# A chunked recurrence's preparation: 64-row products and an inverse that starts from 8x8 blocks

## The chip, the cores and the metric

The kernel runs on one NeuronCore of a Trainium2 chip. A core has a matrix engine (TensorE, PE in the profile, with its weight loads as PEld), VectorE (DVE), ScalarE (ACT), GpSimd (POOL) and SyncE (SP), which here only issues DMAs. The engines work through queues of their own, each in order, and wait for one another by semaphores. The metric is the device time of one execution in microseconds (us); lower is better.

## The reference

Two layers of a hybrid encoder are applied to a prompt of 1024 tokens and to 8 running streams of 16 tokens each, all with 1024 channels. The first layer is an RWKV-7 time mixing, the second a forgetting attention, each followed by a squared-ReLU MLP and a layer norm. The change lies in the time mixing, whose recurrence is, per head (16 heads of 64 channels) and per token:

```
def step(S, inp):
    r_t, d_t, k_t, v_t, av_t, bv_t = inp
    sa = jnp.einsum('bhvk,bhk->bhv', S, av_t)
    S = S * d_t[:, :, None, :] + sa[..., None] * bv_t[:, :, None, :] + v_t[..., None] * k_t[:, :, None, :]
    y_t = jnp.einsum('bhvk,bhk->bhv', S, r_t)
    return S, y_t
...
S_fin, y = lax.scan(step, wkv0.astype(jnp.float32), (tmaj(r), tmaj(decay), tmaj(k), tmaj(v), tmaj(-kk), tmaj(kk * a)))
```

All of it is in float32. The kernel does not go token by token: it takes chunks of 64 tokens, in which the dependence of each token on those before it becomes a triangular system, I - G, of 64 x 64 for each head.

## The kernel before

The 1152 tokens are nine slabs of 128 (slab 0 holds the running streams, slabs 1 to 8 the prompt), two chunks of 64 to a slab. The work runs in three parts. First `project` computes what is local to a token; then comes the recurrence, in which the rest of the first layer for the first tiles runs beside it; then the remaining output product, the MLP, the attention and the second MLP. The change touches the recurrence alone.

For a slab `s` the recurrence has four steps, in functions inside `rwkv`:

- `prep(s)` loads the operands of both chunks. `CE` and `CO` hold the queries and the decayed keys of the even and the odd heads, `BK` what they are multiplied with; even heads lie in partitions 0 to 63 (`E_`), odd heads in 64 to 127 (`O_`). GpSimd clears the other half of `CE` and of `CO` (L449, L450), so that a product over all 128 rows of `BK` gives one head alone: L462, 32 matmuls of 128 columns to a slab, four to a PSUM bank `psG`, of which there are two. VectorE takes one half of a bank with a mask into `ABs` (L463), ScalarE the other half (L468), which GpSimd masks (L469). The even and odd rows of `BK` are then transposed on TensorE into `BT` (L475, out through ScalarE at L476).
- `inv(s)` inverts the 64 x 64 triangles of `ABs`: 32 of them in a slab. Each has four 16 x 16 blocks on its diagonal, 128 in all, one to a partition. VectorE turns them there with four 32x32-block transposes (L489), gathers them (L491, L492), and solves by substitution, 15 steps of a product (L500) and a sum (L501) over squares of 2 x 2 to 16 x 16. Two scalings (L504) and a transpose (L506) put the result back as blocks of 32 x 32 (`XD`; `XT` is its transpose, L511). For the prompt two merges on TensorE follow, each two products of the form X11 G12 X22: the first (L520, L522) fills the block above the diagonal of each 32 x 32 block in tiles of 32 x 32 rows and columns, the second (L546, L548) the same of the 64 x 64 blocks. Between them stand ScalarE copies (L525, L553, L555), a VectorE sum and transpose (L527, L529), and four copies back into `ABs`, two on GpSimd (L533) and two on ScalarE (L535). Slab 0 has blocks of 16 tokens and needs no merge.
- `chain(d, ...)` carries the state through a chunk with small matmuls (L581 to L609), using `CE`, `CO`, `ABs` and `BT`. Its PSUM banks `W0`, `U0`, `W1`, `U1` are the same four, one buffer each, that the merges of `inv` take (`psC`).
- `finish` norms and gates the output.

Beside them run `late` (called as `V(0)` to `V(2)`: values and gates, the matmuls at L34 to L36, L22 to L24 and L156 to L159 on `psA`) and the steps of `ahead` (output product and MLP for three tiles, on `psA` too), which take weights through ScalarE (L52) and VectorE or GpSimd (L53). The program is written in the order P(1), V(0), P(2), inv(1), C(1), inv(2), P(3), ... and a scheduler at compile time sets from this, from its own estimate of durations and from free buffers the order of each engine's queue. Tiles of the inverse share a pool tag `i` with three buffers.

## Time and profile before

| | |
|---|---|
| median of three runs | 3571.83 us (3569.07 to 3585.15) |
| span of the profiled execution, first to last instruction | 3573.1 us |
| PE busy in it | 3371.1 us, 94% |
| PEld busy | 3026.7 us, 85% |
| DVE busy | 1892.1 us, 53% |
| ACT busy | 1435.9 us, 40% |
| POOL busy | 1218.7 us, 34% |
| recurrence, about 425 to 1310 us of the span | 885 us |

The profile gives no separate time for the profiled execution beside its span; the span is 1.3 us over the median of the runs. A busy share is an average over parts with different limits, so it is the recurrence's own windows that count for this change. [...] A float32 matmul stands as two records in the trace, and a record's length includes its latency: what a matmul costs in a stream is the distance from start to start.

### The profile page before, as it was taken

How to read it: one execution, taken by the hardware profiler on the slowest of the kernel's cores; microseconds unless marked ns; L12 is line 12 of the kernel's file. 1: busy time of each engine (PE TensorE's matmuls, PEld its weight loads, DVE VectorE, ACT ScalarE, POOL GpSimd, SP SyncE). 2: the span in 40 equal slices, each digit the busy share in tenths (PEclk: the TensorE clock that was granted, in tenths of full speed). 3: DMA queues.
4: the chain of work that ended last, by engine and by line, in shares of the span. 5: the costliest groups of instructions: out<-in, count | busy, mean ns of one | idle time of the engine just before them, and what ended most of it. 6: DMA issues, size and time to landing. Idle time of an engine off the chain costs nothing.

```text
span 3573.1 us, 65174 instructions
## 1 busy us (share of the span) xinstructions
PE 3371.1 (94%) x26225; PEld 3026.7 (85%) x26225; DVE 1892.1 (53%) x3277; ACT 1435.9 (40%) x2906; POOL 1218.7 (34%) x1061
## 2 busy tenths in 40 slices
PE   7988978899999989999999999999989999999999
PEld 6877877888889888989988987787779899998887
DVE  8988698976674765332225144555456322222225
ACT  5555444443344433323323255555543333232222
POOL 6877765754543444111114011111104111111114
PEclk9988989998999999999999999999999999999999
DMA  4444764664443352212212323323441111111111
GB/s 130 141 137 133 203 165 113 169 184 122 115 119 104 105 198 91 72 59 65 66 59 83 117 74 105 119 90 110 138 150 48 59 48 36 48 45 44 42 42 62
DMA packets 287395, 358.18 MB, mean 100 GB/s; under 512 B 68690, under 2 KB 163948, under 8 KB 287092
## 3 DMA queue, kind: packets, MB, share of 16 engines
q1 hardware_dynamic: 285476, 353.21, 32.8%
q8 instruction: 206, 3.38, 0.4%
q0 software_dynamic: 1152, 0.69, 0.1%
q14 instruction: 97, 0.79, 0.1%
q10 hardware_dynamic: 464, 0.11, 0.0%
HBM read 293.83 MB, written 60.11 MB: 99 GB/s over the span
## 4 chain that ended last, share of the span: by engine, by line
PE 71%; DVE 13%; issue 5%; DMA 5%; POOL 3%; ACT 2%; SPq 1%; DVEq 0%; ACTq 0%; POOLq 0%
PE psy L22 6%; PE psy L24 6%; PE psy L23 6%; PE psz L24 6%; PE psz L23 6%; PE psz L22 6%; PE psA L22 4%; PE psA L23 4%; PE psA L24 4%; PE psO L1170 3%; DVE wl L53 2%; PE psT L1165 2%; PE psA L34 1%; PE psA L36 1%; PE psA L35 1%
## 5 line engine op out<-in xcount | busy, mean ns | idle before, releaser
L53 POOL TENSOR_TENSOR wl<-raw,wh 128x512 fp32r<-128x512 f32 (+1 forms) x291 | 400.1, 1376 | 1709.4 <-ACT wh L52 1656.7
L52 ACT ACTIVATE wh<-raw 128x512 fp32r<-128x512 f32 (+2 forms) x664 | 413.3, 626 | 1041.8 <-PE psy L24 441.4
L53 DVE TENSOR_TENSOR wl<-raw,wh 128x512 fp32r<-128x512 f32 (+2 forms) x373 | 315.9, 850 | 381.8 <-ACT wh L52 378.3
L22 PE MATMUL psz<-AH,wh 128*128 128x384 f32 x1280 | 432.5, 338 | 1.1 <-ACT AH L832 1.1
L24 PE MATMUL psz<-AH,wl 128*128 128x384 f32 x1280 | 432.1, 338 | 0.0
L23 PE MATMUL psz<-AL,wh 128*128 128x384 f32 x1280 | 431.9, 338 | 0.0
L22 PE MATMUL psy<-wh,hh 128*128 128x512 f32 x960 | 379.7, 396 | 0.2 <-DVE X L968 0.2
L24 PE MATMUL psy<-wh,hl 128*128 128x512 f32 x960 | 377.9, 394 | 0.0
L23 PE MATMUL psy<-wl,hh 128*128 128x512 f32 x960 | 377.8, 394 | 0.0
L970 DVE TENSOR_TENSOR X<-X,psy 128x512 f32<-128x512 f32 x210 | 143.9, 685 | 303.8 <-PE psy L24 303.8
L880 DVE TENSOR_TENSOR hl<-r,hh 128x384 fp32r<-128x384 f32 x192 | 115.7, 603 | 342.1 <-ACT hh L879 342.0
L22 PEld LDWEIGHTS psz<-AH,wh 128*128 128x128 f32 x1280 | 240.9, 188 | 2.4 <-ACT AH L832 1.8
L23 PEld LDWEIGHTS psz<-AL,wh 128*128 128x128 f32 x1280 | 241.1, 188 | 0.7
L24 PEld LDWEIGHTS psz<-AH,wl 128*128 128x128 f32 x1280 | 240.8, 188 | 0.0
L22 PE MATMUL psA<-AH,wh 128*128 128x384 f32 x624 | 220.1, 353 | 4.0 <-DVE i L501 2.7
L23 PE MATMUL psA<-AL,wh 128*128 128x384 f32 x624 | 217.4, 348 | 0.0
L24 PEld LDWEIGHTS psy<-wh,hl 128*128 128x128 f32 x960 | 180.4, 188 | 43.2
L22 PEld LDWEIGHTS psy<-wh,hh 128*128 128x128 f32 x960 | 180.5, 188 | 41.3 <-DVE X L968 0.6
L24 PE MATMUL psA<-AH,wl 128*128 128x384 f32 x624 | 214.6, 344 | 0.6 <-DVE wl L53 0.6
L23 PEld LDWEIGHTS psy<-wl,hh 128*128 128x128 f32 x960 | 180.4, 188 | 40.7
L22 PE MATMUL psA<-mh,wh 128*128 128x384 f32 x384 | 141.7, 375 | 38.4 <-DVE fac L323 16.4
L877 ACT ACTIVATE r<-psz 128x384 f32<-128x384 f32 x160 | 77.2, 483 | 185.2 <-PE psz L24 185.2
(390 smaller groups left out, 8466.4 us busy)
## 6 DMA issues: line engine op xcount, KB each, us to landing
raw<-m SPq DMA_DIRECT2D x336, 256.0 KB, 2.7
raw<-m2a SPq DMA_DIRECT2D x64, 256.0 KB, 2.7
sK<-ckT SPq DMA_DIRECT2D x16, 1024.0 KB, 5.5
sV<-cv SPq DMA_DIRECT2D x16, 1024.0 KB, 7.5
x<-xT SPq DMA_DIRECT2D x72, 192.0 KB, 3.4
raw<-w_r SPq DMA_DIRECT2D x48, 256.0 KB, 2.7
raw<-w_k SPq DMA_DIRECT2D x48, 256.0 KB, 2.7
raw<-w_v SPq DMA_DIRECT2D x48, 256.0 KB, 3.8
```

The lines of the kernel that those rows point to most:

```text
L22: nc.tensor.matmul(out, lh, rh, start=i == 0, stop=False)
L23: nc.tensor.matmul(out, lh, rl, start=False, stop=False)
L24: nc.tensor.matmul(out, ll, rh, start=False, stop=i == n - 1)
L34: nc.tensor.matmul(out, lh, rh, start=k == 0 and t % 2 == 0, stop=False, **kw)
L35: nc.tensor.matmul(out, lh, rl, start=False, stop=False, **kw)
L52: nc.scalar.activation(h, r, AF.Copy)
L53: lo[self.i % len(lo)].tensor_tensor(l, r, h.bitcast(F32), op=ALU.subtract)
L877: nc.scalar.activation(r, p, AF.Relu)
L880: nc.vector.tensor_tensor(l, r, h.bitcast(F32), op=ALU.subtract)
L970: nc.vector.tensor_tensor(xs, xs, p, op=ALU.add)
L1165: nc.tensor.transpose(p[:, j], Pms[e][:, (j0 + j) * 128 : (j0 + j) * 128 + 128], cst.ident)
L1170: nc.tensor.matmul(o[q, 0], V[:, j0 + j, q], PTs[e][:, j], start=j0 + j == 0, stop=j0 + j == i, skip_group_check=True)
```

## The change

In `prep` nothing is cleared any more. The products of the even and of the odd heads use the 64 rows of their own (`BK[b]` and `C[b]`), so each is a tile of 64 rows by 128 columns; two PSUM banks are taken at once, and the code issues the matmuls of even and odd heads by turns. The number of matmuls and their columns stay.

In `inv` the substitution starts from 8 x 8 blocks: 256 of them, two to a partition. The diagonal blocks of 32 x 32 are first copied out of `ABs` (`D1`, two copies on ScalarE, two on GpSimd), turned by two transposes of 128 partitions, and gathered in three steps. Seven substitution steps take both blocks of a partition at once. Four scalings and two transposes put the result back. A new merge, for slab 0 too, makes 16 x 16 blocks of them: GpSimd masks `D1` to the 8 x 8 blocks above the diagonal (`N8`), `XD` is transposed, two products of 64 matmuls each (32 x 32 rows and columns, 32 columns of data, four quadrants) run with a ScalarE copy between them, and VectorE adds the result into `XD`. The two merges of before follow unchanged.

```diff
-        rc = pc.tile([128, 578], F32, tag="rc", name="rc")
+        rc = pc.tile([128, 615], F32, tag="rc", name="rc")
         nc.sync.dma_start(rc, I.rconsts)
...
-        own = rc[:, 514:578]
-        mh = [rc[:, 512 + i : 513 + i] for i in range(2)]
+        own = rc[:, 512:576]
+        mh4, mle = ([rc[:, j + i : j + i + 1] for i in range(n)] for j, n in ((576, 4), (580, 3)))
+        m8 = rc[:, 583:615]
...
-                nc.gpsimd.memset(CE[O_], 0.0)
-                nc.gpsimd.memset(CO[E_], 0.0)
...
-                    for C, b, k in ((CE, E_, O_), (CO, O_, E_)):
-                        p = gps().rearrange("p (a b) -> p a b", a=4)
-                        for j in range(4):
-                            kb = hf * 4 + j
-                            nc.tensor.matmul(p[:, j], BK[:, kb], C[:, kb], start=j == 0, stop=j == 3, **kw)
+                    ps = [gps().rearrange("p (a b) -> p a b", a=4) for _ in range(2)]
+                    for j in range(4):
+                        for p, C, b in zip(ps, (CE, CO), (E_, O_)):
+                            nc.tensor.matmul(p[:, j], BK[b, hf * 4 + j], C[b, hf * 4 + j], start=j == 0, stop=j == 3, **kw)
+                    for p, C, b, k in zip(ps, (CE, CO), (E_, O_), (O_, E_)):
...
-            # (I - G)^-1 of the 16 x 16 blocks on the diagonal, a block to a partition
-            G1 = ti_((128, 16, 32))
             ABf = AB.rearrange("p c k t -> p (c k) t")
             qcol = [0, 32, 64, 96]
             qs = [slice(32 * q, 32 * q + 32) for q in range(4)]
+            turned = lambda t, v: t[:, v * 8 : v * 8 + 8].rearrange("p u (h t) -> p t h u", h=4)
+            D1 = ti_((128, 16, 32))
             for q in range(4):
-                nc.vector.transpose(G1[qs[q]], ABf[qs[q], :, qcol[q] : qcol[q] + 32].rearrange("p u (h t) -> p t h u", h=2))
-            Gt = pc.tile([128, 16, 16], F32, tag="Gt", name="Gt")
-            nc.vector.scalar_tensor_tensor(Gt.rearrange("p s t -> p t s"), G1[:, :, 0:16], mh[0], G1[:, :, 16:32], op0=ALU.mult, op1=ALU.add)
-            nc.vector.memset(Gt.rearrange("p a b -> p (a b)")[:, 0 : 256 : 17], 1.0)
-            X = ti_((128, 16, 16))
+                d = ABf[qs[q], :, qcol[q] : qcol[q] + 32]
+                if q % 2:
+                    nc.gpsimd.tensor_copy(D1[qs[q]], d)
+                else:
+                    nc.scalar.activation(D1[qs[q]], d, AF.Copy)
+            G1 = ti_((128, 2, 8, 32))
+            for v in range(2):
+                nc.vector.transpose(G1[:, v], turned(D1, v))
+            N8 = ti_((128, 16, 32))
+            nc.gpsimd.tensor_tensor(N8, D1, m8.unsqueeze(1).broadcast_to([128, 16, 32]), op=ALU.mult)
+            Gt, X = (pc.tile([128, 2, 8, 8], F32, tag=tag, name=tag) for tag in ("Gt", "Xs"))
+            tmp = pc.tile([128, 98], F32, tag="Ts", name="Ts")
+            Gv, Gs = Gt.rearrange("p v t s -> p (v t) s"), [G1.rearrange("p v t s -> p (v t) s")[:, :, i * 8 : i * 8 + 8] for i in range(4)]
+            for i in (2, 1, 0):
+                nc.vector.scalar_tensor_tensor(Gv, Gs[i], mle[i], Gs[3] if i == 2 else Gv, op0=ALU.mult, op1=ALU.add)
+            diag = lambda t: t.rearrange("p v a b -> p v (a b)")[:, :, 0:64:9]
             nc.gpsimd.memset(X, 0.0)
-            nc.gpsimd.memset(X.rearrange("p a b -> p (a b)")[:, 0 : 256 : 17], 1.0)
-            tmp = ti_((128, 256))
-            for s0 in range(14, -1, -1):
-                n = 16 - s0
-                tv = tmp[:, : n * n].rearrange("p (a b) -> p a b", a=n)
-                nc.vector.tensor_tensor(tv, X[:, s0:, s0:], Gt[:, s0, s0:].unsqueeze(1).broadcast_to([128, n, n]), op=ALU.mult)
-                nc.vector.tensor_reduce(X[:, s0:, s0 : s0 + 1], tv, axis=AX.X, op=ALU.add)
+            nc.gpsimd.memset(diag(X), 1.0)
+            for n in range(1, 8):
+                tv = tmp[:, : 2 * n * n].rearrange("p (v a b) -> p v a b", v=2, a=n)
+                r = slice(8 - n, 8)
+                nc.vector.tensor_tensor(tv, X[:, :, r, r], Gt[:, :, r, 7 - n].unsqueeze(2).broadcast_to([128, 2, n, n]), op=ALU.mult)
+                nc.vector.tensor_reduce(X[:, :, r, 7 - n : 8 - n], tv, axis=AX.X, op=ALU.add)
             X2 = ti_((128, 16, 32))
-            for h in range(2):
-                nc.vector.tensor_scalar(X2[:, :, h * 16 : h * 16 + 16], X, mh[h], None, op0=ALU.mult)
+            for h in range(4):
+                nc.vector.tensor_scalar(X2[:, :, h * 8 : h * 8 + 8], X.rearrange("p v t s -> p (v t) s"), mh4[h], None, op0=ALU.mult)
             XD = ti_((128, 16, 32))
-            nc.vector.transpose(XD.rearrange("p u (h t) -> p t h u", h=2), X2)
+            for v in range(2):
+                nc.vector.transpose(turned(XD, v), X2[:, v * 8 : v * 8 + 8])
             kw = dict(skip_group_check=True)
+            XT = ti_((128, 16, 32))
+            nc.vector.transpose(XT, XD)
+            Tm = None
+            for st in range(2):
+                p = cps(1 + 2 * st)
+                for u in range(16):
+                    for q in range(4):
+                        l, r = (N8, XT) if st == 0 else (Tm, XD)
+                        nc.tensor.matmul(p[qs[q], u * 32 : u * 32 + 32], l[qs[q], u], r[qs[q], u], start=u == 0, stop=u == 15, **kw)
+                pv = p.rearrange("p (a b) -> p a b", a=16)
+                if st == 0:
+                    Tm = ti_((128, 16, 32))
+                    nc.scalar.activation(Tm, pv, AF.Copy)
+                else:
+                    nc.vector.tensor_tensor(XD, pv, XD, op=ALU.add)
...
-    c = np.zeros((128, 578), np.float32)
+    c = np.zeros((128, 615), np.float32)
...
+    for i in range(4):
+        c[:, 576 + i] = p % 32 // 8 == i
+    for i in range(3):
+        c[:, 580 + i] = p % 32 // 8 <= i
+    s, t = (p % 32)[:, None], np.arange(32)[None]
+    c[:, 583:615] = (s // 16 == t // 16) & (s % 16 < 8) & (t % 16 >= 8)
```

The scheduler's orders differ from 1,894 matmuls into the program (the first preparation) to the last 4,991, which stand as before. Three places show how.

On VectorE, at the inverse of slab 1, there stood before (`ABs` and `Gt` as above, `xx`, `l`, `wl`, `f`, `wg` and `ev` belong to `late`):

```order
L489 STREAM_TRANSPOSE i<-ABs 32x512 x2
L127 TENSOR_SCALAR f<-f 32x384
L463 TENSOR_TENSOR ABs<-psG,rc 64x512
L145 TENSOR_TENSOR wg<-raw,wg 32x512
L489 STREAM_TRANSPOSE i<-ABs 32x512 x2
L491 SCALAR_TENSOR_TENSOR Gt<-i,rc 128x16x16
L492 MEMSET Gt 128x16
L105 COPY ev<-psA 128x256
L500 TENSOR_TENSOR i<-i,Gt 128x4
```

and now stands:

```order
L497 STREAM_TRANSPOSE i<-i 128x256 x2
L463 TENSOR_TENSOR ABs<-psG,rc 64x512
L504 SCALAR_TENSOR_TENSOR Gt<-i,rc 128x128
L504 SCALAR_TENSOR_TENSOR Gt<-i,rc,Gt 128x128
L463 TENSOR_TENSOR ABs<-psG,rc 64x512
L504 SCALAR_TENSOR_TENSOR Gt<-i,rc,Gt 128x128
L511 TENSOR_TENSOR Ts<-Xs,Gt 128x2
L463 TENSOR_TENSOR ABs<-psG,rc 64x512
L512 TENSOR_REDUCE Xs<-Ts 128x2
```

The inverse's own VectorE instructions go from 39 to 27 in a slab without its later merges, and those of `late` stand between them less often.

On TensorE, at the preparation of slab 1, there stood before (`CE` and `CO` are the even and the odd heads, `psA` is `late`):

```order
L35 MATMUL psA<-wl,h 128x256
L36 MATMUL psA<-wh,l 128x256
L462 MATMUL psG<-CE,BK 128x128 x4
L462 MATMUL psG<-CO,BK 128x128 x4
L462 MATMUL psG<-CE,BK 128x128 x4
L462 MATMUL psG<-CO,BK 128x128 x4
L475 MATMUL psG<-ct,BK 128x64 x8
```

and now stands:

```order
L461 MATMUL psG<-CE,BK 128x128 x4
L35 MATMUL psA<-wl,h 128x256
L36 MATMUL psA<-wh,l 128x256
L461 MATMUL psG<-CO,BK 128x128 x4
L461 MATMUL psG<-CE,BK 128x128 x4
L461 MATMUL psG<-CO,BK 128x128 x4
L475 MATMUL psG<-ct,BK 128x64 x16
```

The code's turns are not kept here: four even matmuls stand in a row, then four odd ones. Over the nine slabs an even matmul stands right beside an odd one, in either order, in 69 places of the queue (0 to 18 of them in a slab), where full turns would give about 280.

On TensorE, where the inverse of slab 1 comes in, there stood before the first merge (L520):

```order
L159 MATMUL psA<-wg,h 128x256
L462 MATMUL psG<-CE,BK 128x128 x4
L462 MATMUL psG<-CO,BK 128x128 x4
L462 MATMUL psG<-CE,BK 128x128 x4
L462 MATMUL psG<-CO,BK 128x128 x4
L475 MATMUL psG<-ct,BK 128x64 x16
L34 MATMUL psA<-wh,h 128x256 x2
L520 MATMUL psC<-i,ABs 32x16 x64
```

and now stand pieces of the new one (L529):

```order
L461 MATMUL psG<-CO,BK 128x128 x4
L529 MATMUL psC<-i 32x32 x6
L475 MATMUL psG<-ct,BK 128x64 x4
L156 MATMUL psA<-wh,h 128x256
L157 MATMUL psA<-wl,h 128x256
L158 MATMUL psA<-wh,l 128x256
L159 MATMUL psA<-wg,h 128x256
```

The new merge's first product stands before transposes of slab 2 and before matmuls of `late`, which can't pass it while it waits. Between its two products, and again before the next merge, some 15 to 34 other matmuls stand in most slabs. Over the recurrence, neighbours in TensorE's queue whose tiles differ in rows or columns go from 483 to 575.

## Rows read from the trace of the kernel before

**Rows 1.** The page: span.

```profile
span 3573.1 us, 65174 instructions
```

**Rows 2.** Windows: stretch, us, busy PE PEld DVE ACT POOL (instructions), PEclk, DMA share, GB/s.

```profile
425.00:1310.00 885.00, 805.46 (x10560) 734.87 (x10560) 661.39 (x1184) 372.63 (x744) 479.34 (x450) 0.93 0.49 137
463.00:729.00 266.00, 226.80 (x3464) 204.72 (x3464) 241.95 (x420) 113.92 (x242) 171.32 (x182) 0.87 0.54 147
729.00:1310.00 581.00, 548.02 (x6885) 502.99 (x6883) 394.90 (x732) 243.87 (x472) 278.62 (x237) 0.96 0.43 127
```

**Rows 3.** Windows of the inverses' substitutions: the first, and nine summed.

```profile
463.00:498.00 35.00, 21.77 (x149) 19.63 (x148) 33.68 (x59) 14.84 (x30) 26.64 (x29) 0.81 0.61 172
...
sum 372.00, PE 329.69 PEld 299.83 DVE 344.24 ACT 155.65 POOL 202.93; mean PE 36.63 PEld 33.31 DVE 38.25 ACT 17.29 POOL 22.55
```

**Rows 4.** Waits of PE, 463 to 729 us: total, times, longest.

```profile
PE psC L520 <- DVE i L511: 9.2, 4, 5.6
```

**Rows 5.** DVE groups of the inverse, 425 to 1310 us: count, busy, mean ns, idle before.

```profile
L500 DVE TENSOR_TENSOR i<-i,Gt 128x4 f32<-128x4 f32 (+4 forms) x135 | 61.5, 455 | 2.7
...
L489 DVE STREAM_TRANSPOSE i<-ABs 32x512 f32<-32x512 f32 x36 | 38.4, 1068 | 0.5
L501 DVE TENSOR_REDUCE i<-i 128x2 f32<-128x4 f32 (+4 forms) x135 | 34.4, 255 | 2.8
...
L506 DVE STREAM_TRANSPOSE i<-i 128x512 f32<-128x512 f32 x9 | 9.9, 1102 | 0.1
...
L491 DVE SCALAR_TENSOR_TENSOR Gt<-i,rc 128x256 f32<-128x256 f32 x9 | 8.9, 992 | 0.1
...
L504 DVE TENSOR_SCALAR i<-i,rc 128x256 f32<-128x256 f32 x18 | 8.5, 512 | 0.1
...
L511 DVE STREAM_TRANSPOSE i<-i 128x512 f32<-128x512 f32 x8 | 5.6, 698 | 0.1
```

**Rows 6.** Two of those groups by shape, 425 to 1310 us.

```profile
L500 DVE TENSOR_TENSOR i<-i,Gt 128x36 f32<-128x36 f32 x9 | 3.7, 410 | 0.2
...
L501 DVE TENSOR_REDUCE i<-i 128x6 f32<-128x36 f32 x9 | 1.7, 190 | 0.2
```

**Rows 7.** Timeline of PE at merges of slab 6: start, us, instruction.

```profile
1014.71 0.34 PE L24 MATMUL psA<-AH,wl 128*128 128x384 f32 x1
1014.98 1.26 PE L520 MATMUL psC<-i,ABs 32*32 32x16 f32 x128
1016.17 0.45 PE L22 MATMUL psA<-AH,wh 128*128 128x384 f32 x1
...
1024.47 1.31 PE L546 MATMUL psC<-i,ABs 32*32 32x32 f32 x64
```

**Rows 8.** Timeline of PE at a preparation.

```profile
486.68 1.16 PE L462 MATMUL psG<-CE,BK 128*128 128x128 f32 x8 [0.51 <-ACT CE L468]
487.71 1.16 PE L462 MATMUL psG<-CO,BK 128*128 128x128 f32 x8
```

**Rows 9.** Timeline of PE at transposes: both halves by turns, then one alone.

```profile
742.68 1.02 PE L475 MATMUL psG<-ct,BK 64*128 64x64 f32 x16
...
820.13 0.71 PE L475 MATMUL psG<-ct,BK 64*128 64x64 f32 x8
```

**Rows 10.** Timeline of PE where the tile's shape changes.

```profile
1046.49 0.28 PE L35 MATMUL psA<-wl,hh 128*128 128x256 f32 x1
1046.60 0.28 PE L36 MATMUL psA<-wh,hl 128*128 128x256 f32 x1
1046.81 0.46 PE L475 MATMUL psG<-ct,BK 64*128 64x64 f32 x4
```

**Rows 11.** Groups of POOL and ACT, 425 to 1310 us, columns as in rows 5.

```profile
L449 POOL MEMSET CE<- 64x1024 f32 x18 | 17.1, 948 | 1.0
...
L533 POOL COPY ABs<-i 32x512 f32<-32x512 f32 x18 | 12.2, 679 | 10.6 <-DVE i L527 6.0 <-DVE i L506 2.8 <-DVE st L631 1.0
...
L535 ACT ACTIVATE ABs<-i 32x512 f32<-32x512 f32 x18 | 11.3, 626 | 17.2 <-DVE i L527 13.3 <-DVE i L506 3.8
```

More of the change, by code (lines that the diff above doesn't have):

```diff
@@ L1411, in _prep @@
         c[:, i * 256 : i * 256 + 256] = np.concatenate([np.where(e, ab, ba), np.where(e, ba, ab)], 1)
-    for i in range(2):
-        c[:, 512 + i] = p % 32 // 16 == i
     t = np.arange(64)[None]
-    c[:, 514:578] = p[:, None] == t // 16 * 32 + t // 16 % 2 * 16 + t % 16
+    c[:, 512:576] = p[:, None] == t // 16 * 32 + t // 16 % 2 * 16 + t % 16
+    for i in range(4):
[4 more added lines that the diff above has]
+    c[:, 583:615] = (s // 16 == t // 16) & (s % 16 < 8) & (t % 16 >= 8)
     o["rconsts"] = c
```

## The prediction

> **What bounds the kernel now.** I looked first at the page's engine shares: TensorE is busy 94% of the 3573.1 us [rows 1], which says little, as the change touches the recurrence alone. So the windows come next. In the recurrence's 885 us TensorE is busy 805, 91%, at a mean clock of 0.93 [rows 2]. The reader is to see that this is a mean of two stretches with different limits. From 463 to 729 us, with four of the nine inverses, VectorE is busy 242 of 266 us (91%) and TensorE 227 (85%), at a clock of 0.87. TensorE loses there 39 us idle and about 0.13 x 227 = 29 us to the lower clock, 68 us in all, and VectorE is what it waits for. From 729 to 1310 us it is the other way round: TensorE 548 of 581 us (94%) at 0.96, VectorE 395 (68%). What is lost there is 33 us idle and 0.04 x 548 = 22 us of clock.
>
> Windows laid on the substitutions alone (from the first L489 to L506, nine of them) sum to 372 us, in which VectorE is busy 344, or 93%; in the first, TensorE has work for 22 of 35 us only, at a clock of 0.81 [rows 3]. The list of TensorE's waits names the inverse at its head: L520 waited 9.2 us in four places for the transpose L511 that ends it [rows 4]. The groups by line give the inverse's own VectorE time: 61.5 + 38.4 + 34.4 + 9.9 + 8.9 + 8.5 = 161.6 us, 18.0 us a slab [rows 5]. That is the largest single block on the engine that sets the early stretch.
>
> **The change part by part.** VectorE in the inverse. The four turns of 32 partitions x 512 (1.07 us each) become two of 128 x 256: half the columns, so I take 0.55 each, 1.1 us. Gathering: three steps of 128 columns; half of L491's 0.99 or of L504's 0.51 for 256 [rows 5], I take 0.4, together 1.2. Substitution: seven pairs over 2 to 98 elements; the pair at 36 elements takes 0.41 + 0.19 [rows 6], so 7 x 0.6 = 4.2, against (61.5 + 34.4)/9 = 10.7 before. Scalings 4 x 0.26 = 1.0, the two transposes back 1.1, the new transpose `XT` 0.7 as L511, the sum into `XD` over as many columns 0.7 too. That is 10.0 against 18.0: 8 us less a slab, 72 us in all. Bounds: were each halved piece to cost what the whole does, the four halved kinds would cost 2.1 + 3.0 + 2.0 + 2.2 and the slab 14.9, 3 us less (27 in all); were they as short as their sizes allow and the small substitution steps cheaper still, some 10 us less (94).
>
> TensorE, new merge: 18 products of 64 matmuls, 128 records each. No row shows 32 data columns in four quadrants, but two stand close. [...] L546, 32 columns in two quadrants, has 64 records in 1.31 us less the last one's latency, which I estimate at 0.19, so a quadrant is free again after 1.12/32 = 35 ns [rows 7]. Four records at L520's pace, 1.26 less that latency over 128 = 8.5 ns, fill just these 35 ns, so the product keeps L520's length: 18 x 1.29 = 23 us. Bounds: 0 where TensorE would have idled anyway, 46 where all of it falls to the lower clock.
>
> TensorE, 64-row products. A record of L462 takes 1.03/8 = 0.13 us [rows 8], and its columns don't change. Two tiles of 64 rows do run side by side: 16 transposes of both halves, partly by turns, take 1.02 us, where eight of one half take 0.71 and eight more at 0.06 would make 1.2 [rows 9]. But only neighbours gain. In the order there are 69 places where an even matmul touches an odd one, each worth one record: 69 x 0.13 = 9 us. Full turns would give some 36. On the other side each change of the tile's shape costs: L36 follows L35 after 0.11 us, the 64*128 transpose follows L36 after 0.21 [rows 10]. Of the 92 further changes about 36 belong to the new products and are in their 1.29; 56 x 0.1 = 6 us remain, since L462 had the shape of its neighbours and its successor hasn't. So the two-heads part is worth 3 us of TensorE, and the whole change adds about 20.
>
> [...]
>
> POOL and ACT. Four clearings of 0.95 us a slab go, 34 us in all; two copies of 0.68 [rows 11] and one mask of 512 columns come, which I put at 1.4, twice a copy of 32 x 512; about 1 us a slab less. ScalarE gets two copies of 0.63 and one out of PSUM of about 0.6: 1.9 a slab, 17 us. Both engines are busy around half of the recurrence [rows 2], so I count neither. If that cover is gone, it is the copies `D1` that show: 1.4 us at the head of each inverse, 12 us. The list behind rows 4 names no clearing among TensorE's waits, so its end ends no stall.
>
> The wait that is added: the first product of the merge waits for `XT`, the second for ScalarE's copy, the next merge for VectorE's sum. Behind each stand matmuls of `late` or `ahead` and, in slab 1, transposes of slab 2, on which ScalarE and then the next inverse wait. With 15 to 34 other matmuls in between, at about 0.12 us each, some 2 to 4 us cover a copy of 0.6 and a sum and transpose of 1.4, so I count nothing; uncovered it would be about 1 us a slab.
>
> The sum. Early stretch: VectorE's load falls by 4 x 8 = 32 us; TensorE at full clock needs 227 - 29 + 4 x 2.2 = 207 of the 266 and doesn't bind. Not all of the 32 comes through, as DMAs also hold this stretch (share 0.54), so two thirds: 22 us less, with the added TensorE work inside it. Late stretch: TensorE's 5 x 2.2 = 11 us come in full, and VectorE's 40 us get back a fifth of the 55 lost: 11. Net nothing. What is late next in the early stretch is the matmuls and weight loads of `late`. The profiled execution: 3573.1 - 20 = 3553 us; the median stands 1.3 lower, so 3552.
>
> **The rivals.**
> First: VectorE sets more than I think. Then the early 32 us come in full and the late stretch gains half of 40 less 11, so 41 us less: 3531. For it speaks the 93% in rows 3; against it TensorE's 94% late.
> Second: the change brings nothing to measure, since DMA and order hold the early stretch. With 10 us gained early and 11 lost late: 3573. For it: only one wait of 9.2 us is plainly the inverse's.
> Third, the slower side: TensorE is the bound and the new merge stands in its queue. The 20 us of added work land in full, and the waits of the new products, uncovered by about 1 us a slab, add 9: 3601. It decides from the point at which less than 20 us of the 68 us lost early comes back. For it: 91% busy over the recurrence, pieces of the new merge ahead of slab 2's transposes in the queue. Against it: the early stretch, where TensorE has slack.
> Fourth: the quadrants of the new merge don't run beside one another. Then a product takes 128 x 35 ns = 4.5 us, 18 x 3.4 = 61 us more than forecast: 3613.
>
> **How the numbers follow.** The forecast, 3552, has 0.45, with a range of its own from 3538 to 3566; the first rival 0.18, the second 0.20, the third 0.13, the fourth 0.04. 0.5% is 18 us, about what this kernel's runs differ by. Faster than 3554: all of the first, somewhat over half of the forecast and a little of the second, 0.46. Slower than 3590: most of the third and the fourth, 0.14. The rest, 0.40, is within. The range, 3522 to 3592, cuts off the lower fourth of the first rival and most of the third and fourth, under 2 in 10.
>
> **What would show it.** VectorE's lines of the inverse should sum to about 90 us instead of 162, most of it in the seven substitution steps. From 463 us on, the four early inverses and what goes with them should end some 22 us sooner, with TensorE's clock over 0.9. The new products should take about 1.1 us from first to last record at the full clock, and L461's even and odd records should start within 10 ns of each other only where the queue has them side by side. The forecast is wrong if TensorE waits over 1 us a slab at L529, if VectorE's 72 us are gone and the early stretch is as long as before, or if the late one shrinks.

## The result and the profile after

The changed kernel takes 3626.09 us (median of 4 runs, 3622.53 to 3628.2), the kernel before 3574.38 (4 runs, 3569.07 to 3585.15): a ratio of 1.0147, with an interval from 1.0129 to 1.0165. It is 52 us slower. The forecast was 3552 us, 3522 to 3592, and "slower" had the smallest chance.

The windows of the kernel after, over the stretches of [rows 2], columns as there:

```profile
425.00:1310.00 885.00, 813.85 (x12435) 731.52 (x12434) 584.89 (x1018) 373.77 (x734) 444.76 (x430) 0.85 0.45 129
463.00:729.00 266.00, 230.58 (x4339) 204.06 (x4339) 206.37 (x356) 110.61 (x229) 157.55 (x174) 0.77 0.48 136
729.00:1310.00 581.00, 550.21 (x7896) 497.83 (x7896) 353.68 (x629) 247.17 (x474) 262.52 (x226) 0.90 0.40 118
```

The trace records TensorE's granted clock at two levels, and PEclk is its mean over a stretch: 1.0 and 0.5 before, 0.949 and 0.5 in this one profile, where the others have 1.0 for the upper level; matmuls behind the recurrence last as long as before (338 ns for the 384 columns of `psz` in both). With that, the share of the early stretch at the lower level is (0.949 - 0.77) / 0.449 = 40%, where 0.87 before is 26%. VectorE has become lighter, 206 instead of 242 us. TensorE is busier and still gets less done, since it runs at the lower level for longer: by the record of the granted clock, 191 us of the recurrence instead of 123. The recurrence, from 425 us to the last matmul of its chain, takes 905 us instead of 856.

The first substitution, 20 us instead of the 35 of [rows 3]:

```profile
469.00:489.00 20.00, 14.88 (x77) 12.87 (x75) 19.27 (x33) 5.86 (x12) 18.81 (x24) 0.58 0.59 170
```

VectorE's groups of the new inverse, 425 to 1362 us (it was [rows 5]). They sum to 103.7 us instead of 161.6, with the sum into `XD` (L535) and the new transpose `XT` (L522) among them:

```profile
L511 DVE TENSOR_TENSOR Ts<-Xs,Gt 128x2 f32<-128x2 f32 (+6 forms) x63 | 28.7, 455 | 1.6
L512 DVE TENSOR_REDUCE Xs<-Ts 128x2 f32<-128x2 f32 (+6 forms) x63 | 12.2, 193 | 1.5
L515 DVE TENSOR_SCALAR i<-Xs,rc 128x128 f32<-128x128 f32 x36 | 11.9, 387 | 0.2
L504 DVE SCALAR_TENSOR_TENSOR Gt<-i,rc,Gt 128x128 f32<-128x128 f32 x18 | 11.8, 658 | 0.4
L497 DVE STREAM_TRANSPOSE i<-i 128x256 f32<-128x256 f32 x18 | 10.8, 632 | 4.9 <-POOL i L492 4.1 <-PE psC L576 0.7
L518 DVE STREAM_TRANSPOSE i<-i 128x256 f32<-128x256 f32 x18 | 10.2, 645 | 0.2
L522 DVE STREAM_TRANSPOSE i<-i 128x512 f32<-128x512 f32 x9 | 6.3, 697 | 0.0
L535 DVE TENSOR_TENSOR i<-psC,i 128x512 f32<-128x512 f32 x9 | 6.1, 683 | 2.6 <-PE psC L529 2.5
L504 DVE SCALAR_TENSOR_TENSOR Gt<-i,rc 128x128 f32<-128x128 f32 x9 | 5.7, 630 | 0.2
```

TensorE's timeline at one product of the new merge, and at a place where products of the two heads follow each other by turns. Two heads' records start together, and 0.11 us later the next two:

```profile
633.66 1.29 PE L529 MATMUL psC<-i 32*32 32x32 f32 x128
...
1100.34 0.27 PE L461 MATMUL psG<-CE,BK 64*128 64x128 f32 x1
1100.34 0.27 PE L461 MATMUL psG<-CO,BK 64*128 64x128 f32 x1
1100.45 0.27 PE L461 MATMUL psG<-CE,BK 64*128 64x128 f32 x1
1100.45 0.28 PE L461 MATMUL psG<-CO,BK 64*128 64x128 f32 x1
```

TensorE's waits at the preparation and the merges, 425 to 1362 us: total, times, longest. The first of the older merges no longer waits for the inverse's transpose, as L520 did for L511 [rows 4]; the products now wait for ScalarE's copies out of the banks (2.1 and 0.5 us before), and the older merges for their own copy (L553) and transpose (L557), once each:

```profile
PE psG L461 <- ACT CE L468: 9.7, 6, 2.6
PE psC L550 <- ACT i L553: 4.5, 1, 4.5
PE psC L574 <- DVE i L557: 4.3, 1, 4.3
PE psG L461 <- ACT CO L468: 3.7, 4, 2.0
...
PE psC L529 <- DVE Stmp L628: 0.3, 1, 0.3
```

Where the recurrence's 49 us come from can be added up by charging each TensorE record with the time from its start to the next one's, less waits, and taking half of what lies at the lower level as the clock's price (in the two kernels with streams below, 600 records of 64 rows take 67.26 us at a clock of 1.00 and 400 take 85.70 at 0.50, 112 and 214 ns each):

```
                                  before    after
new merge, at full clock             0       25.6
all other records, at full clock   725.8    723.8
half of the records' time at 0.5    54.3     84.9
waits                               76.2     71.2
```

So 26 us are the new merge, 31 us the clock, and waits and other records give 7 back. All that VectorE was spared gave TensorE almost no time.

### The profile page after: what moved, and what is told of

It is laid out like the page before. It is cut to its first block, busy times and chain, and to the rows that moved or that the text cites. A ratio compares the mean times of both kernels' runs of the same rounds, so it can differ in the third digit from the quotient of the medians.

```text
span 3626.4 us, 69718 instructions
## 1 busy us (share of the span) xinstructions
PE 3432.4 (95%) x28529; PEld 3070.1 (85%) x28529; DVE 1847.1 (51%) x3169; ACT 1455.7 (40%) x2933; POOL 1201.4 (33%) x1052
## 4 chain that ended last, share of the span: by engine, by line
PE 66%; DVE 6%; DMA 3%; issue 3%; POOL 1%; ACT 1%; SPq 0%; DVEq 0%; ACTq 0%; POOLq 0%
PE psy L22 6%; PE psy L24 6%; PE psy L23 6%; PE psz L24 6%; PE psz L23 6%; PE psz L22 6%; PE psA L23 3%; PE psA L22 3%; PE psA L24 3%; PE psO L1198 3%; PE psT L1193 2%; PE psA L34 1%; PE psA L36 1%; PE psA L35 1%; PE psS L1178 1%
```

## The experiments

Each version below is the kernel before or after with the edit shown. The first four weigh the merge (A) against the new preparation, with its two banks and its longer time at the lower clock (B). C then says that products of 64 rows keep the clock down; D, that the order and the two banks held together make the price; E, that it is the missing clearings. The table gives all timed versions. "Lower, all" is the time at the lower level in the whole kernel, (1 - mean granted clock) x span x 2, averaged over a version's runs (of the changed kernel without the one that records 0.949); "in rec." is the same by the clock's record of the profiled execution in the recurrence, and "waits" TensorE's there, so these two stand on one execution each.

```
version        rows cleared merge   ratio [95%]            lower,all in rec. waits
before          128  yes     no     1                       247-262   123     76
e14_bt128       128  yes     no     0.9977 [0.9967,0.9986]    216      96     79
e10_invonly     128  yes     left out 0.9971 [0.9956,0.9986]  242      96     68
e12_loaded      128  no      no     1.002  [1.001,1.003]      245     123     85
e5_rows128      128  yes     no     1.0065 [1.0047,1.0083]    268     143     86
e2_inv          128  yes     yes    1.0068 [1.0053,1.0083]    246     102     73
e3_nomerge       64  no      left out 1.0005 [0.9992,1.0017]  274     154     65
e9_cleared       64  yes     no     1.0046 [1.0031,1.0061]    315     171     82
e13_rows64c      64  yes     no     1.0098 [1.0081,1.0116]    317     212     77
e6_onebank       64  no      no     1.01   [1.0069,1.0131]    306     167     79
e1_prep          64  no      no     1.0123 [1.0106,1.014]     336     225     81
e15_after_bt128  64  no      yes    1.0101 [1.0079,1.0122]    286     150     72
after            64  no      yes    1.0147 [1.0129,1.0165]    324     191     71
e7_chained       64  no      yes    1.0162 [1.0147,1.0177]    321     198     91
e4_turns         64  no      yes    1.0404 [1.0387,1.0421]    416     266    162
```

**The two parts apart.** e1_prep is the kernel before with the changed preparation; e2_inv is the changed kernel with the preparation of before.

```diff
-for C, b, k in ((CE, E_, O_), (CO, O_, E_)):      # e1_prep: these go, and the clearings
-    p = gps()...; for j: matmul(p[:, j], BK[:, kb], C[:, kb], ...)
+ps = [gps()... for _ in range(2)]
+for j in range(4):
+    for p, C, b in zip(ps, (CE, CO), (E_, O_)):
+        matmul(p[:, j], BK[b, hf * 4 + j], C[b, hf * 4 + j], ...)
```

> The kernel before with the new preparation alone (64-row products, two banks at once, nothing cleared); the inverse is that of before. Even and odd matmuls touch in 74 places of its queue. Theory A (the price of the change is the new merge's TensorE time, start to start 35 us in the changed kernel's recurrence; the preparation is worth next to nothing): 3574 to 3584 us. Theory B (the price is the new preparation: products that wait for both banks, 11 us more in the changed kernel, and a longer time at the lower clock): 3595 us or more.

> The changed kernel with the preparation of before (128-row products of cleared halves); the inverse from 8x8 blocks stays. Theory A: 3605 to 3620 us, most of the 52 us. Theory B: under 3595 us. If the parts add up, this and the preparation alone sum to the 52 us.

e1_prep took 3617.95 us against 3574.45, e2_inv 3596.65. So the part forecast as 3 us of gain costs 43 by itself, the inverse 22; together they cost 52, less than the sum. For e2_inv neither theory's range fits. The early stretch of e1_prep (columns of [rows 2]) shows where: TensorE as busy as before, the clock at 0.72.

```profile
463.00:729.00 266.00, 228.58 (x3009) 201.25 (x3008) 212.10 (x386) 99.25 (x209) 133.34 (x154) 0.72 0.49 129
```

At full clock e1_prep's recurrence needs 720.2 us of TensorE instead of 725.8, the small gain that was forecast; half of its time at the lower level is 100.4 instead of 54.3.

**The merge.** e3_nomerge is the changed kernel without the 8x8 merge (its mask, transpose, products, copy and sum, so part of each 16 x 16 block of the inverse is left out); e10_invonly the same with the preparation of before.

```diff
-N8 = ...; XT = ti_(...); nc.vector.transpose(XT, XD)
-for st in range(2): ... matmul(p[qs[q], ...], l[qs[q], u], r[qs[q], u], ...) ...
```

> The changed kernel without the new merge of 8x8 blocks (mask, transpose, both products, the copy and the sum are left out, so the blocks of 16 are not complete and the output isn't the reference's). VectorE's shorter substitution stays. Theory A: the merge's 35 us of TensorE go, and its share of the lower clock: 3580 to 3592 us. Theory B: 3600 us or more. If VectorE's relief of 8 us a slab were worth what I had forecast, this would be under 3555 us.

> The kernel before with the inverse from 8x8 blocks and without its new merge on TensorE (so the 8x8 blocks below the diagonal are left out: part of the computation): VectorE's relief by itself, with the preparation of before. As the prediction's main forecast had it, that relief is worth 22 to 33 us when TensorE gets nothing more to do: 3540 to 3552. If TensorE is what sets the recurrence, it is worth almost nothing: 3565 to 3578. Together with the changed kernel's inverse on the same preparation (1.0068) it gives the merge's full price: 25 us if it is TensorE's time at full clock and nothing else.

e10_invonly is the test of VectorE's relief, and it is worth 9 us (3564.93 against 3574.22, by the interval 5 to 16), though without the merge's own transpose and sum VectorE is spared some 70 us, 161.6 to 91. Its early stretch has VectorE at 213 us instead of 242, but TensorE at 235 instead of 227:

```profile
463.00:729.00 266.00, 235.45 (x3709) 210.91 (x3710) 213.41 (x371) 127.06 (x264) 178.22 (x195) 0.90 0.53 153
```

The merge costs 1.0068 - 0.9971, about 35 us, with 128-row products, and 51 us with 64-row ones (3574.97 to 3626.09), though its records take 25 to 26 in both. With the 64 rows the merge brings 37 us more at the lower level of the recurrence (154 to 191), with 128 rows 6 more (96 to 102). e3_nomerge, at 3574.97, lies below both theories: the new preparation costs 12 us beside this inverse (1.0005 - 0.9971), 30 with the merge (3596.65 to 3626.09) and 43 beside the inverse of before.

**Turns.** e4_turns keeps each bank pair's eight matmuls together as one uninterrupted block; e7_chained only fixes their order of issue.

```diff
+with tc.tile_critical():                            # e4_turns, around the eight matmuls
+    prev = matmul(...), each issued after prev      # e7_chained
```

> The changed kernel with each bank pair's eight product matmuls kept in the turns of the code (one block for the scheduler): even and odd touch in 254 places instead of 69. If each place is worth a record (0.13 us), 24 us less of TensorE: 3602 us. If the turns put the halves side by side but the time is lost to the lower clock or to waits for two banks, 3615 to 3630 us.

> The changed kernel with one edit: the eight product matmuls of a pair of banks are queued in the written order (even, odd, even, ...) by an edge that sets the order of issue alone, so other work may still stand between them: 220 touching places instead of 69, and no blocks that wait as a whole. Theory C: the products cost some 25 us less TensorE time at full clock, but the time at the lower clock stays as long as in the changed kernel (191 us) or gets longer: 3595 to 3630. Theory D (the order is what costs): the price of the preparation goes with it, 3570 to 3590. If the waits of the blocks were what made the kernel with blocks slow (3718), this one is at least 80 us faster than that one under both.

Turns do save what they promise: the products' cost at full clock falls from 65.7 us to 39.6 in e4_turns (254 touching places) and to 51.9 in e7_chained (220). But e4_turns' block waits as a whole for things that have nothing to do with the preparation, as the head of its waits shows (425 to 1410 us), and e7_chained loses 20 us to more waits and stays as long at the lower level as the changed kernel. Both were slower than it, e7_chained within the intervals; e4_turns is far outside both of its forecasts.

```profile
PE psG L461 <- DMA raw<-g1b: 17.8, 1, 17.8
PE psG L461 <- POOL xx L78: 12.8, 2, 7.8
PE psG L461 <- DMA vg<-v: 9.6, 3, 5.3
```

**Rows, banks, clearings.** Five edits of the preparation of before.

```diff
e5_rows128:  both banks asked for together, matmuls by turns in the code, still BK[:, kb], C[:, kb], cleared
e6_onebank:  bank by bank; -BK[:, kb], C[:, kb]  +BK[b, kb], C[b, kb]; no clearings
e13_rows64c: e6_onebank with the clearings kept
e9_cleared:  e1_prep with the clearings kept
e12_loaded:  e1_prep with
-    nc.sync.dma_start(CE[E_], scr.ca[ci, 0:64]); matmul(..., BK[b, ...], C[b, ...])
+    nc.sync.dma_start(CE, scr.ca[ci]);           matmul(..., BK[:, ...], C[:, ...])   # CO likewise
```

> The kernel before with one edit: the two product banks of a half are asked for together and their matmuls stand in turn in the code, still 128 rows of contraction, still cleared. In the queue the two banks then follow each other much as before (22 touching places of the two banks' matmuls, 30 before). Theory C (TensorE's clock falls for longer when the products contract over 64 rows): nothing changes here, 3574 +-8 us, about 123 us of the recurrence at the lower clock level. Theory D (the price of the new preparation comes from the two banks held together and from the order that this gives, not from the rows): slower by a large part of the 43 us that the preparation cost, 3590 or more.

> The kernel before with one edit: each product contracts over its own head's 64 rows, and the two clearings on GpSimd go; the banks follow each other as before (22 touching places), so nothing runs side by side. Theory C: slower by most of the preparation's 43 us, 3600 to 3620, with over 180 us of the recurrence at the lower clock level (before 123), and the same TensorE time at full clock. Theory D: like the kernel before, 3574 +-8 us, or a few us less for the clearings that are gone.

> The kernel before with the new preparation (products of 64 rows, both banks together), but with GpSimd's two clearings per chunk kept, which nothing reads. It differs from the 128-row version with both banks together (1.0065, 143 us of the recurrence at the lower clock level) in the rows alone, and from the one without clearings (1.012, 225 us) in the clearings alone. Theory C (rows): 3605 to 3620, 180 us or more at the lower level. Rival (the clearings, which hold the preparation back so that it stands differently to the rest): 3585 to 3597, about 145 us.

> The kernel before with the new preparation, but the tiles of coefficients loaded whole (both heads' rows, by the same DMAs with twice the bytes) and the products over all 128 rows, nothing cleared: each product is the sum of both heads' (another result), with no work of GpSimd's clearings and no products of 64 rows. Theory C (rows): the price of the preparation without clearings (1.012) goes: 1.000 to 1.007, under 150 us of the recurrence at the lower level, though the two banks no longer run side by side, which gave 5 to 7 us. Rival E (the clearings held the preparation back to a better place, and rows matter little): 1.009 to 1.015, 170 us or more at the lower level. A loss by the doubled loads would show as TensorE waiting for them at the products' line.

> The kernel before with its products over 64 rows, bank by bank, the clearings kept: against the same without clearings (1.010, 167 us at the lower level) only the clearings differ, against the kernel before the rows alone (beside what the order makes of it). Theory C: 1.006 to 1.013, 150 us or more at the lower level. Rival E: 0.998 to 1.004, 130 us or less.

Three pairs differ in the rows alone, e12_loaded and e1_prep beside this in the bytes loaded (and e12_loaded's products are sums over both heads). From 128 to 64 rows:

```
pair                       time    lower,all
before -> e13_rows64c     +35 us      +70 us
e12_loaded -> e1_prep     +37         +91
e5_rows128 -> e9_cleared   -7         +47
```

So C holds for the clock in every pair, and for the time in two of three. Also from e2_inv to the changed kernel and from e10_invonly to e3_nomerge the time at the lower level rises, by 78 and 32 us; no version of 128 rows has over 268 us and none of 64 rows under 274. The early stretches of e12_loaded, then e13_rows64c:

```profile
463.00:729.00 266.00, 225.88 (x3339) 201.47 (x3337) 238.39 (x415) 112.76 (x239) 152.53 (x166) 0.88 0.58 160
```

```profile
463.00:729.00 266.00, 231.26 (x3103) 204.92 (x3102) 210.87 (x384) 105.06 (x220) 153.39 (x174) 0.76 0.47 130
```

And of e5_rows128, then e9_cleared:

```profile
463.00:729.00 266.00, 222.63 (x3529) 200.91 (x3530) 233.72 (x410) 112.02 (x233) 168.97 (x182) 0.85 0.50 139
```

```profile
463.00:729.00 266.00, 228.04 (x3115) 202.00 (x3112) 228.74 (x388) 107.10 (x225) 160.14 (x176) 0.78 0.49 136
```

In this last pair half of the recurrence's time at the lower level grows by 17 us in the profiled executions, but the products need 61.7 us at full clock instead of 71.0, as 113 records start within 10 ns of one of the other head.

E is out where the banks follow each other: e6_onebank and e13_rows64c cost 1.010 and 1.0098, without and with clearings, in time as C had it (e6_onebank's 167 us at the lower level stay under C's 180). With both banks held it isn't. e9_cleared differs from e1_prep in the clearings alone, is 28 us faster (1.0046, 1.0123), and lies where the rival had put it (3585 to 3597), not where C had. Why clearings that nothing reads should help was not found out.

D holds in part: e5_rows128 changes neither rows nor work and costs 23 us, as D had forecast. Its order is another one, too: in the trace the two heads' products touch in 89 places, against 30 before, where the expectation has 22. Its waits at the products are 18.6 us instead of 8.6, 6.4 of them for ScalarE's copies instead of 2.6; some 20 us more at the lower level make another 10.

**The clock by itself.** Two kernels put stages of products behind the end of the kernel before, each stage after 200 full matmuls (128 rows x 256 columns); the last four of e11_probe2 stand each after a wait of some 21 us instead. Each kernel was run once, and the operands are constants that soon shrink towards zero, for all row counts alike.

```diff
+rows128: for i: matmul(P0[:, 0:128], A, B)          # 128 rows
+rows64:  for i: matmul(P0[:, 0:128], A[E], B[E])    # 64 rows
+turns:   for i: rows64's, then matmul(P1[:, 0:128], A[O], B[O])
+e11_probe2, after each group of 4 or 8: nc.scalar.activation(A, P0[:, 0:128], Copy, scale=1e-6)
```

> The kernel before with streams of matmuls by themselves behind its end, each after 200 full ones (f32r, 128 rows x 256): 300 of 128 rows x 128 columns; 300 of 64 rows; 300 pairs of 64 rows in turn on both halves of the rows; 900 rounds of four 32x32 products on the four quadrants; 600 rounds of two 64x64 products. Theory C: the granted clock holds its upper level in the 128-row stream and falls to the lower one in the 64-row stream; in turns it holds longer than in the 64-row stream. Theory D: the upper level in all of these streams, so that the loss is made by what stands around the products in the recurrence. The four quadrants' stream shows the cost of one 32x32 product when nothing else is queued (8 to 9 ns a record if the rows of the changed kernel are its rate, 25 ns and more if the four do not run together).

> The kernel before with stages behind its end. Six stages of 40 groups of products, each group followed by a wait for ScalarE (about 0.4 us): 4 and then 8 products of 128 rows, of 64 rows, and 4 or 8 pairs of 64 rows in turn, each stage after 200 full matmuls. Then four streams after a wait of over 10 us: 200 full ones (f32r, 128 rows x 256), 200 products of 128 rows, 200 of 64 rows, 200 pairs in turn. Theory C, in the form that the streams without waits leave to it: with waits between them the 64-row groups fall to the lower level and the 128-row groups hold the upper one, and after a wait the 64-row stream takes longer to come back to the upper level, or never does, while 128 rows, full ones and pairs come back within 10 us. Rival: rows make no difference in either, and the clock goes by the waits alone.

Windows on e8_probe's streams without waits: 300 products of 128 rows, 300 of 64 rows, 300 pairs in turn, the quadrants, the 64x64 products. Columns: stretch, us, TensorE busy (records), granted clock, DMA share, GB/s.

```profile
3616.86:3684.13 67.27, 67.27 (x600) 1.00 0.01 1
3709.45:3776.71 67.26, 67.26 (x600) 1.00 0.00 1
3802.04:3869.30 67.26, 67.26 (x1200) 1.00 0.01 2
3895.02:4102.32 207.30, 107.27 (x7200) 0.51 0.02 4
4129.63:4199.84 70.21, 70.21 (x2400) 1.00 0.02 4
```

After full matmuls an unbroken stream of 64 rows holds a clock of 1.00, against C as first put; 300 pairs take the 67.26 us of 300 single products. The quadrants' stream doesn't settle their cost: for 100 us of it TensorE stood idle without a wait that the profile shows ("issue"), and the clock was 0.51.

Windows on e11_probe2, same columns: 40 groups of four products of 128 rows, of 64 rows, four pairs; then the same three with eight; then, each after the long wait, 200 full ones, 200 of 128 rows, 200 of 64 rows, 200 pairs.

```profile
3602.01:3665.26 63.25, 46.34 (x320) 1.00 0.00 1
3690.71:3788.45 97.74, 81.10 (x320) 0.51 0.00 1
3815.25:3952.08 136.83, 119.90 (x640) 0.52 0.00 1
3979.13:4078.13 99.00, 82.07 (x640) 1.00 0.00 1
4103.58:4269.72 166.14, 149.22 (x640) 0.51 0.00 1
4296.53:4451.58 155.05, 138.41 (x1280) 1.00 0.01 1
4473.11:4499.67 26.56, 26.56 (x200) 0.90 0.00 1
4520.61:4568.19 47.58, 47.58 (x400) 0.94 0.00 1
4589.07:4674.77 85.70, 85.70 (x400) 0.50 0.00 1
4695.65:4742.77 47.12, 47.12 (x800) 0.95 0.01 2
```

This bears C out, apart from the recurrence's order. With the same waits between them (17 us in sum), groups of 128 rows run at 1.00 throughout and groups of 64 rows at 0.51. And a stream of 64 rows that begins at 0.5 stays there, without a pause, for all of its 85.7 us, where 128 rows, full matmuls and pairs in turn come back early in theirs (means of 0.94, 0.90 and 0.95). But rows don't decide alone: groups of four pairs run at 0.52, groups of eight at 1.00. In the trace most of a group's pairs are not side by side, as a run of one half's records comes first and a run of the other's last (13 of 16 each in a group of eight), and still these 64-row products hold the clock.

In the recurrence the clock fell about as often in e1_prep as before (20 times, 17 before) and in e13_rows64c as often (17), but e1_prep's longest stays were 41, 31 and 31 us and e13_rows64c's 51, 34 and 27, where before none was over 14; a stay lasts 11.3 and 12.4 us on average, 7.2 before. So the stays grew there, not the number of falls, which fits the stream that begins at 0.5.

**From the other side.** The transposes of the update's rows also work on 64 rows. e14_bt128 and e15_after_bt128 make them whole, in the kernel before and after.

```diff
-for par, q in ((0, E_), (1, O_)):
-    for kb in range(8): transpose(p[:, kb * 64 : kb * 64 + 64], BK[q, kb], ident[q, q])
+for h4 in range(2):
+    for j in range(4): transpose(p[:, j * 128 : j * 128 + 128], BK[:, h4 * 4 + j], ident)
```

> The kernel before with its other half-row work made whole: the rows of the state's update are turned by 8 transposes of 128 rows x 128 columns a chunk instead of 16 of 64 rows x 64 columns, into the same banks. If rows hold the clock down after a wait, this brings it back sooner: 0.990 to 0.998, under 110 us at the lower level; the instructions take the same time in sum (16 x 76 ns against 8 x 150 ns at most). If the order decides more than rows do: anything from 0.993 to 1.008, as other small edits of the preparation gave. The one version here that might beat both kernels and leaves nothing out.

> The changed kernel with the same 128-row transposes. Theory C: 5 to 20 us less than the changed kernel (1.009 to 1.013 against before), under 180 us at the lower level (191 before). Otherwise 1.012 to 1.020.

e14_bt128 takes 3559.12 us against 3568.72, with some 30 us less at the lower level: the one version that beats both kernels and leaves nothing out. e15_after_bt128 takes 3602.46, some 16 us off the changed kernel's price. In e14_bt128 the late stretch holds 0.98 (0.96 in [rows 2]):

```profile
463.00:729.00 266.00, 225.54 (x3290) 202.86 (x3289) 240.26 (x419) 114.30 (x244) 169.75 (x185) 0.87 0.53 148
729.00:1310.00 581.00, 542.50 (x7001) 499.58 (x6999) 415.66 (x754) 251.56 (x483) 285.99 (x240) 0.98 0.44 132
```

The transposes' own cost at full clock fell too, from 22.0 to 17.6 us, so not all of the 10 us is the clock's.

## Why the prediction was wrong

**The step that failed** is "So the two-heads part is worth 3 us of TensorE". The count behind it was right: 75 records start within 10 ns of one of the other head, at 0.11 us each, and the products need 65.7 us at full clock instead of 68.6. What it left out is the clock those products leave behind. I priced each edit by durations at the level the trace happened to have, as if the 29 and 22 us lost to the clock in the two stretches [rows 2] were a property of the stretch. They hang on the products themselves. By e1_prep the term is 43 us of loss, and in its trace half of the time at the lower level, 100.4 us instead of 54.3, covers all of it. By e12_loaded 37 of the 43 go with the 64 rows; with the clearings kept (e9_cleared) the loss shrinks to 15, so the size hangs on the order as well, while the longer time at the lower level comes with the rows in every pair.

**"Two thirds of 32 early, a fifth of 55 late".** The forecast took 33 us for VectorE's relief; e10_invonly measured 9. The relief itself was there, 58 us of the 72 forecast and within the bounds: the gathering took 17.5 us, as L504 needs 0.66 us for 128 columns where I took 0.4, and the rest was close. But VectorE busy for 91% of the early stretch was not TensorE waiting for VectorE. The inverse stood at the head of TensorE's waits with only 9.2 us [rows 4], and e10_invonly's waits fall by 8 (76 to 68). The second rival had put the gain there, at 10 us.

**The new merge.** No run shows the 1.29 us that the forecast takes as L520's length (its 128 records take 1.26 [rows 7]). The runs showed about that for the new product: 1.29 us with the last record's latency, 128 records 8.5 ns apart, so the fourth rival is out, and the records' 26 us stand against 23 forecast. That they would cost nothing late and hide early was wrong: they came in full, and 35 us with what goes with them.

**POOL, ACT and waits.** ScalarE was counted at nothing. TensorE's waits for its copies at the products rose from 2.6 to 13.4 us; e5_rows128, with both banks held and 128 rows, has 6.4, so the banks explain part of it. The waits for the new merge itself stayed covered (L529 waited 0.3 us for data), while L550 and L574 waited 4.5 and 4.3 us once each. All waits together fell by 5 us.

**The rivals.** The fourth, 3613, is nearest in number by luck, as its mechanism is out. Of the others the third, with TensorE as the bound and the merge in full, comes nearest: it gave 3601, and e2_inv, the inverse alone, measured 3597. But its 9 us of waits were not seen, and it lacked the clock, as did every other case; with 31 us for it and without those waits the sum would have been 3623. The sign I named for a wrong forecast was seen: VectorE is relieved, and the tenth chunk's first product starts at 759 us instead of 731.

**What stays open.** Why the parts' prices (43 and 22) don't add up to 52 isn't settled, nor why the preparation's is 12, 30 or 43 us by what stands beside it. The order differs in each version: by e5_rows128 order and banks alone move the time by 23 us, and by e9_cleared two clearings a chunk by 28. That 64 rows lengthen the time at the lower clock is shown; what the rows alone cost in time ran from nothing to 37 us.

## What to carry to other kernels

Price an edit of TensorE's work also by what it does to the clock: halving the rows of short products cost no TensorE time at full clock here (720.2 us in e1_prep, 725.8 before) and still up to 1% (37 us, e12_loaded to e1_prep), where waits stand between them (a clock of 0.51 in the groups with waits, 1.00 in the unbroken stream). A busy engine is the bound only as far as another waits for it: here some 70 us of VectorE's time spared gave 9, so read the wait's own total before spending the busy time saved. And if two half-row pieces can be one whole one, as the transposes here, that may gain twice (in e14_bt128 22.0 to 17.6 us at full clock, and some 30 us less at the lower level).

## What the runs showed of the hardware

The same products at 64 rows ran at a granted clock of 1.00 in an unbroken stream that began there (e8_probe), at 0.50 in one that began at 0.5, and at 0.51 in groups with short waits (both e11_probe2). At 128 rows the clock was 1.00 in the stream and in the groups, and came back in the stream that began low (0.94 over it). Groups of eight pairs of 64 rows, most of them not side by side, held 1.00 too, groups of four ran at 0.52. The profile's busy time alone does not order these: 128-row groups hold 1.00 at 46.3 us busy of 63.3, and the 64-row stream stands at 0.50 with 85.7 of 85.7.
